# Turning layer inputs and heads in 32x32 blocks on the vector engine, in a two-layer hybrid decoder trunk

## The chip, the cores and the metric

One core of one Trainium2 chip. The metric is the time of one execution on the device, in microseconds (us); of several runs the median counts. Times of single instructions come from one profiled execution. Engines by their names in the profile: PE is the matmul engine, PEld its weight loads, DVE the vector engine, ACT the scalar engine, POOL GpSimd, SP the engine whose queue issues all DMAs here.

## What is computed

A trunk of two layers over x of 2048 rows and 1024 columns, float32. Each layer, cut to what matters:

```
proj = x @ w_in                                   # 1024 -> 3608 columns
dn_q, dn_k, dn_v, dn_z, dn_b, dn_a, g_q, g_k, g_v, g_z, g_r = split(proj)
q, k, v = silu(causal_conv4(dn_q, dn_k, dn_v)); q, k = l2norm(q) / sqrt(128), l2norm(k)
o_dn  = gated_delta_rule(q, k, v, g(dn_a), sigmoid(dn_b))      # 4 heads of 128
o_dn  = rms_norm(o_dn, per head) * dn_norm_g * silu(dn_z)
log_f = log_sigmoid(g_r @ gla_gate_w2 + gla_gate_b) / 16
o_gla = gated_linear_attention(g_q / 8, g_k, g_v, log_f)       # 4 heads, keys 64, values 128
o_gla = rms_norm(o_gla, per head) * gla_norm_g * silu(g_z)
y = concat(o_dn, o_gla) @ w_out                   # 1024 -> 1024
x = layer_norm(alpha * x + y) * ln_g + ln_b       # alpha = 4 ** 0.25
```

Both recurrences carry a state from row to row; the delta rule is computed in chunks of 128 rows with the inverse of a triangular matrix per chunk and head.

## The kernel before

**Tiling.** Each layer is worked off in two halves of 1024 rows (L1341), each half in two blocks of 512 rows (`b`), each block in four chunks of 128 rows (`c`). So there are four halves in all, and eight chunks in each. Every operand of a projection is kept as two float32r parts, `hi` (the rounded value) and `lo` (the rest), and a projection is three products: hi x hi, hi x lo, lo x hi. `proj_group` (L715) makes 24 matmuls of 128x512 for a group of 128 output columns and a block; a half has 24 such groups (four each of delta-rule queries, keys and values, eight of gates, four of the other queries and keys) for each of two blocks. `out_half` (L1287) makes 24 for one chunk and one half of the 1024 output columns.

**The order of the work.** The kernel is first recorded. `Recorder.order` (L238) then simulates the five engines with costs from `_cost` (L477), hands each engine the ready operation with the lowest key (its place in the program, less a lift that a `+n` in `PLAN` gives to a stage), and emits one fixed order for each engine. `HOP` (L465) is the time that the planner counts from the end of an operation on one engine to its use on another. Operations recorded with `either` (copies, scalings, and `subtract` and `product`) go to the engine that would end them sooner. `SLOTS` (L552) gives the number of buffers by tag; a buffer is used again when its last reader is done. In `PLAN` (L558), q, a and b are stages of the linear attention, d, k, i, m, v, y and r those of the delta rule (decay, keys, inverse, its completion, values, queries, recurrence), w the second pair's values, g gates; the digits are the head or pair, and the block. `m4` has 5 buffers of 128x1024 words, `wh` and `wl` 3 each, `xt` 4 (each `hi` or `lo` of a block's inputs, and of half the output weights).

**The inputs.** `load_row` (L726) brings 128 rows as they are, rows on partitions. `prep_xt` (L731) turns them: 8 transposes per chunk on PE against the identity matrix `ident`, into two PSUM banks of tag `tr`; ACT rounds each bank to `hi`, DVE subtracts to `lo`. Partition p of column block k is then contraction row 128k + p, and the weights are loaded likewise (`load_w`, L694; `load_wo`, L1260).

**The heads.** `dn_rec` (L1223, the delta rule) and `gla_long` (L957) leave a head of a block as rows on partitions, scaled by its norm. `finish_head` (L1033) turns it with 4 transposes on PE into a PSUM bank of tag `ch`, and scales it by the gain (per partition by then) into `oT`. `gate` (L1041) projects the head's gate, takes its SiLU, multiplies `oT` by it and sends the product to the DRAM buffer `og`. `split_o` (L1272) brings a chunk of all eight heads back with columns on partitions and splits it to `hi` and `lo` for `out_half`; for chunks 0 to 2 it does so in three pieces, the last of which is head 3 alone, and the matmuls take the heads in the order 4, 5, 6, 7, 0, 1, 2, 3 (L1285). The last three gates are worked off behind the plan (L1430 to L1436), for block 0 and then for block 1.

**The inverse.** `dn_invert` (L1108) builds the 32x32 diagonal blocks of the inverses of all eight chunks of a head on DVE, in `Tb`, with group, chunk and block on partitions. They pass through the DRAM buffer `ud` (L1141 to L1144) to get the layout in which `dn_merge` (L1150) completes the inverse on PE (tag `mg`).

**The recurrence** of a head walks its chunks one by one: two matmuls with the state `Sd`, one with `rr`, two with `vn`, and between them steps on DVE and ACT. Projections of other stages fill PE in between, as the order has it.

Of the kernel before, what the change touches and what calls it, by code (L numbers as in the profile page):

```python
# [464 lines left out]
HOP = {"tensor": 55.0, "vector": 35.0, "scalar": 35.0, "gpsimd": 110.0, "sync": 60.0}  # L465
# [11 lines left out]
def _cost(o, outs, ins):  # L477
# [4 lines left out]
    if o.eng == "tensor":  # L482
# [5 lines left out]
        if lhs.dt == F32R:  # L488
            o.takes = max(w / 2.4 + 14.0, 110.0)
            if o.mode != "r":  # L490
                o.takes = 430.0
        elif o.name == "transpose":
            o.takes = 110.0
        else:
            o.recs = 2
            o.takes = {"32x32": 26.0, "64x32": max(18.0, 0.42 * w), "128x32": max(18.0, 0.42 * w), "64x64": 62.0, "128x64": 113.0,
                       "64x128": 127.0}.get(o.mode, 2 * max(111.5, w * 0.85))
# [37 lines left out]
    else:  # L535
# [17 lines left out]
         "s1": 16, "Sc": 3, "nd": 2, "ud": 2, "og0": 2, "og1": 2, "decd": 2, "bst": 4, "gr": 2, "U32": 1, "T32": 1, "Nd": 2}  # L553
BANKS = {"pj": 2, "tr": 3, "ch": 2, "mg": 1}
LEVELS_MASK = (16, 8, 4, 2, 1)
WHOLE, PARTS = ((0, 8),), ((4, 8), (0, 3), (3, 4))
# [6 lines left out]
def hymba_trunk(ctx: ExitStack, tc, x, w_in, conv_w, dn_a_log, dn_dt_bias, gla_gate_w2, gla_gate_b,  # L563
# [469 lines left out]
    def finish_head(o, gain):  # L1033
        pt = PS([P, NC, P], "ch")
        for c in range(NC):
            nc.tensor.transpose(pt[:, c, :], o[:, c, :], ident)
        oT = T([P, BLK], "m2")
        scaled(oT, pt.rearrange("p c t -> p (c t)"), gain)
        return oT

    def gate(w, xtb, oT, dst):  # L1041
        acc = proj_group(w, xtb)
        y = row2()
        nc.scalar.activation(y, acc, AF.Silu)
        product(oT, oT, y)
        nc.sync.dma_start(dst, oT)
# [61 lines left out]
    def dn_invert(st):  # L1108
# [114 lines left out]
    def dn_rec(h, b, st):  # L1223
# [33 lines left out]
        return finish_head(o, gd)  # L1257


    def load_wo(l, n):  # L1260
        hi = T([P, KT, BLK], "xt", F32R)
        lo = T([P, KT, BLK], "xt", F32R)
        for k in range(0, KT, 2):
            ks = slice(k, k + 2)
            raw = T([P, 2, BLK], "m4")
            nc.sync.dma_start(raw, w_out[l][k * P:(k + 2) * P, n * BLK:(n + 1) * BLK]
                              .rearrange("(k p) c -> p k c", p=P))
# [17 lines left out]
    HEADS = (4, 5, 6, 7, 0, 1, 2, 3)  # L1285

    def out_half(o2, wo, n, y, st):  # L1287
        (oh, ol), (wh, wl) = o2, wo
        acc = PS([P, BLK], "pj")
        for k in HEADS:  # L1290
            nc.tensor.matmul(acc, oh[:, k, :], wh[:, k, :], start=(k == HEADS[0]), stop=False)
            nc.tensor.matmul(acc, oh[:, k, :], wl[:, k, :], start=False, stop=False)
        for k in HEADS:
            nc.tensor.matmul(acc, ol[:, k, :], wh[:, k, :], start=False, stop=(k == HEADS[-1]))
# [16 lines left out]
    def out_proj(l, so, do, src, dst, og, wo, o2):  # L1311
# [7 lines left out]
        for c, n in ((0, 0), (1, 0), (2, 0), (0, 1), (1, 1), (3, 0), (2, 1), (3, 1), (4, 0), (4, 1), (5, 0), (5, 1),  # L1319
                     (6, 0), (7, 0), (6, 1), (7, 1)):  # L1320
            if n == 0:
# [3 lines left out]
                if c not in o2:  # L1325
                    o2[c] = split_o(c, og, WHOLE)
# [7 lines left out]
    for l in range(depth):  # L1334
# [6 lines left out]
        for hf in range(n_half):  # L1341
# [8 lines left out]
            og = [DR([8, P, BLK], f"og{b}") for b in range(NB)]  # L1350
# [4 lines left out]
            if l == 0 and hf == 0:  # L1355
                with lifted(600):
                    early = {0: load_row(src, 0)}
            wv0 = load_v(l, 0, True)
            for b in range(NB):
                with lifted(150):  # L1360
                    xt.append(prep_xt(lambda c: early.pop(b * NC + c, None) or load_row(src, so + b * BLK + c * P)))
# [23 lines left out]
            oT = {}  # L1385

            def g2(p, b):
                os_ = gla_long(gl[p, b], v[p, b], Sg[p])
                for h in range(2):
                    oT[4 + 2 * p + h, b] = finish_head(os_[h], gg)  # L1390

            def gates(e):
                w = load_group(l, (GZ0 + P * (e - 4)) if e > 3 else Z0 + P * e)
                for b in range(NB):
                    gate(w, xt[b], oT[e, b], og[b][e])
# [14 lines left out]
            def rec_block(h, b):  # L1410
                oT[h, b] = dn_rec(h, b, dn[h])
# [18 lines left out]
            z = [(e, load_group(l, Z0 + P * e)) for e in (1, 2, 3)]  # L1430
            for e, w in z:
                gate(w, xt[0], oT[e, 0], og[0][e])
            wo = [load_wo(l, 0)]
            o2 = {0: split_o(0, og, PARTS)}
            for e, w in z:
                gate(w, xt[1], oT[e, 1], og[1][e])  # L1436
            for c in (1, 2):
                o2[c] = split_o(c, og, WHOLE if c > 2 else PARTS)
            wo.append(load_wo(l, 1))
            out_proj(l, so, do, src, dst, og, wo, o2)  # L1440
# [27 lines left out]
```

## Time and profile before

| | |
|---|---|
| runs shown (3) | 2171.54, 2171.9, 2174.57 us; median 2171.9 |
| profiled execution | 2170.34 us |
| its span, first to last instruction | 2168.6 us |
| granted clock of PE | 0.998 |
| busy: PE, PEld, DVE, ACT, POOL | 98%, 82%, 65%, 53%, 23% of the span |
| moved by DMA | 215.40 MB, 279267 packets |

How to read it: a group row gives line, engine, operation, the tiles written and read by the program's names (`m` stands for the buffers of both `m2` and `m4`, `s` for small ones), the shape and the count; behind the bar, the time in which the group was busy, the mean duration of one instruction in ns, and the idle time of its engine just before them with what ended it. Every instruction is emitted at L433, so tiles, not lines, tell the groups apart. A transpose on PE reads as a matmul that has `ident` as an operand. A float32 matmul that is not a transpose counts twice, for it is made of two records. A timeline row gives the start and the duration in us; merged instructions have a count. Matmuls overlap, so the spacing of their starts and not the duration tells what each takes from PE.

### The profile page before, as it was taken

How to read it: one execution, taken by the hardware profiler on the slowest of the kernel's cores; microseconds unless marked ns; L12 is line 12 of the kernel's file. 1: busy time of each engine (PE TensorE's matmuls, PEld its weight loads, DVE VectorE, ACT ScalarE, POOL GpSimd, SP SyncE). 2: the span in 40 equal slices, each digit the busy share in tenths (PEclk: the TensorE clock that was granted, in tenths of full speed). 3: DMA queues.
4: the chain of work that ended last, by engine and by line, in shares of the span. 5: the costliest groups of instructions: out<-in, count | busy, mean ns of one | idle time of the engine just before them, and what ended most of it. 6: DMA issues, size and time to landing. Idle time of an engine off the chain costs nothing.

```text
span 2168.6 us, 45520 instructions
## 1 busy us (share of the span) xinstructions
PE 2122.9 (98%) x17426; PEld 1779.1 (82%) x17426; DVE 1408.5 (65%) x3311; ACT 1157.3 (53%) x3253; POOL 495.2 (23%) x877
## 2 busy tenths in 40 slices
PE   8999999999999999999999999999999999999998
PEld 7887878788998788878888878887889887888787
DVE  4567777656456777755645677776564567777556
ACT  4676756441457675643145767565315576656520
POOL 3342112111134211211113421111111341212110
PEclk9999999999999999999999999999999999999999
DMA  4222332373221332236322143324732213332461
GB/s 140 70 61 81 105 86 67 102 220 122 89 69 51 96 110 71 72 109 215 123 87 60 50 115 96 81 57 119 223 112 81 67 48 108 96 80 57 126 190 58
DMA packets 279267, 215.40 MB, mean 99 GB/s; under 512 B 69828, under 2 KB 225800, under 8 KB 279048
## 3 DMA queue, kind: packets, MB, share of 16 engines
q1 hardware_dynamic: 279048, 212.48, 33.3%
q8 instruction: 137, 2.24, 0.4%
q14 instruction: 82, 0.67, 0.1%
HBM read 166.23 MB, written 46.20 MB: 98 GB/s over the span
## 4 chain that ended last, share of the span: by engine, by line
PE 85%; DMA 5%; DVE 5%; ACT 2%; issue 1%; POOL 1%; DVEq 0%; SPq 0%; POOLq 0%
PE pj L433 65%; PE ch L433 9%; PE tr L433 8%; DMA ud<-Tb 4%; PE mg L433 2%; DMA U<-ud 1%; ACT m L433 1%; DVE m L433 1%; DVE kq L433 1%; DVE wl L433 1%; DVE tmp L433 1%; DVE R L433 0%; POOL s L433 0%; DVE s L433 0%; DVE Tb L433 0%
## 5 line engine op out<-in xcount | busy, mean ns | idle before, releaser
L433 PE MATMUL pj<-xt,wh 128*128 128x512 f32 x4096 | 1090.5, 402 | 2.1 <-ACT wh L433 2.1
L433 PEld LDWEIGHTS pj<-xt,wh 128*128 128x128 f32 x4096 | 742.9, 189 | 141.3 <-ACT wh L433 3.0
L433 PE MATMUL pj<-xt,wl 128*128 128x512 f32 x2048 | 568.4, 401 | 0.0
L433 PEld LDWEIGHTS pj<-xt,wl 128*128 128x128 f32 x2048 | 374.4, 189 | 69.0 <-issue 0.2
L433 PE MATMUL pj<-wh,xt 128*128 128x256 f32 (+1 forms) x1024 | 196.6, 290 | 1.5 <-ACT wh L433 1.5
L433 POOL TENSOR_TENSOR s<-s,mhalf 128x4 f32<-128x4 f32 (+2 forms) x80 | 103.3, 1292 | 334.3 <-DVE s L433 333.5
L433 PEld LDWEIGHTS pj<-wh,xt 128*128 128x128 f32 x1024 | 162.2, 190 | 2.4 <-ACT wh L433 1.9
L433 ACT CAST wh<-wr 128x1024 fp32r<-128x1024 f32 (+2 forms) x116 | 118.0, 1024 | 86.0 <-PE pj L433 62.6
L433 DVE SCALAR_TENSOR_TENSOR kq<-raw,cw,kq 128x512 f32<-128x512 f32 x192 | 146.5, 765 | 3.7
L433 DVE TENSOR_TENSOR wl<-wr,wh 128x512 fp32r<-128x512 f32 (+2 forms) x170 | 119.4, 733 | 21.3 <-ACT wh L433 11.8
L433 PE MATMUL pj<-wl,xt 128*128 128x280 f32 (+1 forms) x512 | 131.3, 289 | 0.9 <-DVE wl L433 0.5
L433 DVE TENSOR_TENSOR m<-m,m 128x256 f32<-128x256 f32 (+1 forms) x244 | 114.4, 490 | 19.8 <-ACT m L433 5.5
L433 DVE SCALAR_TENSOR_TENSOR m<-m,pj 128x512 f32<-128x512 f32 x64 | 43.9, 685 | 121.9 <-PE pj L433 121.9
L433 ACT CAST wh<-m 128x1024 fp32r<-128x1024 f32 (+3 forms) x56 | 37.3, 679 | 159.3 <-PE pj L433 148.8
L433 POOL MEMSET m<- 128x512 f32 (+1 forms) x160 | 79.0, 508 | 90.1 <-PE tr L433 56.7
L433 POOL TENSOR_TENSOR wl<-wr,wh 128x512 fp32r<-128x512 f32 (+2 forms) x42 | 61.2, 1466 | 167.7 <-ACT wh L433 126.7
L433 PEld LDWEIGHTS pj<-wl,xt 128*128 128x128 f32 x512 | 97.6, 191 | 1.6 <-DVE wl L433 0.8
L433 POOL COPY halo<-raw 128x3 f32<-128x3 f32 x96 | 20.4, 213 | 341.7 <-ACT raw L433 299.0
L433 PEld LDWEIGHTS ch<-Sd,kq 128*128 128x128 f32 x512 | 78.4, 190 | 23.6 <-DVE Sd L433 13.4
L433 ACT COPY m<-m 64x256 f32<-64x256 f32 (+1 forms) x198 | 78.0, 411 | 23.1 <-PE tr L433 11.3
L433 PE MATMUL ch<-Sd,kq 128*128 128x128 f32 x512 | 87.1, 278 | 3.2 <-DVE Sd L433 2.7
L433 DVE SCALAR_TENSOR_TENSOR Sd<-Sd,eg,ch 128x128 f32<-128x128 f32 x128 | 44.2, 345 | 69.2 <-PE ch L433 68.0
(193 smaller groups left out, 3407.9 us busy)
## 6 DMA issues: line engine op xcount, KB each, us to landing
wr<-in_w_in_dram SPq DMA_DIRECT2D x104, 512.0 KB
m<-decd SPq DMA_DIRECT2D x64, 256.0 KB
og<-m SPq DMA_DIRECT2D x64, 256.0 KB
m<-in_w_out_dram SPq DMA_DIRECT2D x32, 512.0 KB
m<-og SPq DMA_DIRECT2D x20, 512.0 KB
m<-in_x_dram SPq DMA_DIRECT2D x16, 512.0 KB
m<-gr SPq DMA_DIRECT2D x32, 256.0 KB
decd<-m SPq DMA_DIRECT2D x32, 256.0 KB
```

Source lines behind the costliest of these rows:

```text
L433: getattr(getattr(self.nc, o.eng), o.name)(*[real(a) for a in o.args], **{k: real(a) for k, a in o.kw.items()})
```

## The change

Inputs, heads and weights meet in another order of the 1024 contraction rows: partition p of column block k now holds row 8p + k (`rows_of`). The inputs come in four DMAs for each chunk, one for each 256 columns, onto 32 partitions each: partition 32a + t holds, for each of the four groups of 32 rows, columns 256a to 256a + 255 of row t of the group. One `transpose` instruction on DVE turns all 32x32 blocks of a chunk (`turned`); it reads every eighth word and writes in sequence. ACT's rounding and the subtraction read its output, and the subtraction may now be on DVE or POOL. PE's transposes of the inputs are gone.

Heads go to DRAM as they are (`finish_head` is one DMA), into `og`, by pairs; gates, with the gain multiplied in, go to a DRAM buffer of their own, `zg`. `split_o` loads a chunk's heads in the form of the inputs, turns them likewise on DVE, loads the chunk's gates, multiplies, and splits. Heads and gates no longer wait for each other before DRAM, the pieces of `split_o` are gone, and the matmuls take the column blocks in order. PE's transposes of the heads are gone.

`ud` gets an order in which the write is contiguous in each partition. The planner counts 300 ns instead of 55 for a hop to PE, and 42 ns for a matmul of 64 by 32; `PLAN` has another order and other lifts.

```diff
-HOP = {"tensor": 55.0, "vector": 35.0, "scalar": 35.0, "gpsimd": 110.0, "sync": 60.0}
+HOP = {"tensor": 300.0, "vector": 35.0, "scalar": 35.0, "gpsimd": 110.0, "sync": 60.0}
...
-            o.takes = {"32x32": 26.0, "64x32": max(18.0, 0.42 * w), "128x32": max(18.0, 0.42 * w), "64x64": 62.0, "128x64": 113.0,
+            o.takes = {"32x32": 26.0, "64x32": 42.0, "128x32": max(18.0, 0.42 * w), "64x64": 62.0, "128x64": 113.0,
...
-PLAN = ("q0 w d1 a00 b00 a01 d0+400 b01 q1+50 a10 b10 k0 v0 g4+50 a11 i0 g5 b11 m0+50 y0 r00 k1 d2 y1 d3 "
-        "i1 g7 r01+50 g6 k2 m1 v1 r10 r11+600 v2 i2 k3 y2 m2 r20 r21 v3 y3 i3+50 m3+200 r30 r31+250 g0+100")
+LAST = 1, 2, 3
+PLAN = ("q0+50 w a00 d0+200 b00+50 d1 a01 q1 a10 b01 d2 k0 v0 b10+100 g4 a11 i0 b11+700 y0+100 g5 m0 k1+500 d3+200 r00 k2 "
+        "y1 r01 v1 i1 m1+50 k3 g6 r10 y2 i2 m2+400 v2+450 r11+1050 r20+50 r21 v3+100 g7+400 i3+150 g0 m3+650 y3+50 r30+300 r31+250")
...
+    def rows_of(src):
+        return src.rearrange("(p k) c -> p k c", p=P)
+
+    def turned(raw):
+
+
+        out = T([P, NC, KT, 32], "m4")
+        nc.vector.transpose(out, raw.rearrange("p b (i k) -> p b k i", k=KT))
+        return out.pattern(0, [(32, KT), (32 * KT, NC), (1, 32)])
...
-                nc.sync.dma_start(raw[:, :, at:at + w],
-                                  src[k0 * P:(k0 + n_k) * P, c0:c0 + w].rearrange("(k p) c -> p k c", p=P))
+                nc.sync.dma_start(raw[:, :, at:at + w], rows_of(src)[:, k0:k0 + n_k, c0:c0 + w])
...
-    def load_row(src, t):
-        row = T([P, D], "m4")
-        nc.sync.dma_start(row, src[t:t + P, :])
-        return row
+    def load_rows(src, t):
+        raw = T([P, NC, 2 * P], "m4")
+        for a in range(4):
+            nc.sync.dma_start(raw[32 * a:32 * a + 32], src[t:t + P, 256 * a:256 * a + 256].rearrange("(b t) e -> t b e", b=4))
+        return raw
...
         for c in range(NC):
-            row = rows(c)
-            pts = []
-            for kk in range(0, KT, 4):
-                pt = PS([P, 4, P], "tr")
-                for j in range(4):
-                    nc.tensor.transpose(pt[:, j, :], row[:, (kk + j) * P:(kk + j + 1) * P], ident)
-                pts.append(pt)
-            for kk, pt in zip(range(0, KT, 4), pts):
-                h = hi[:, kk:kk + 4, c * P:(c + 1) * P]
-                nc.scalar.copy(h, pt)
-                nc.vector.tensor_tensor(out=lo[:, kk:kk + 4, c * P:(c + 1) * P], in0=pt,
-                                        in1=h.bitcast(F32), op=ALU.subtract)
+            xt = turned(rows(c))
+            parts = lambda t: t[:, :, c * P:(c + 1) * P].rearrange("p k (b t) -> p k b t", b=4)
+            nc.scalar.copy(parts(hi), xt)
+            subtract(parts(lo), xt, parts(hi).bitcast(F32))
...
-    def finish_head(o, gain):
-        pt = PS([P, NC, P], "ch")
-        for c in range(NC):
-            nc.tensor.transpose(pt[:, c, :], o[:, c, :], ident)
-        oT = T([P, BLK], "m2")
-        scaled(oT, pt.rearrange("p c t -> p (c t)"), gain)
-        return oT
-
-    def gate(w, xtb, oT, dst):
+    def finish_head(o, dst):
+        nc.sync.dma_start(dst.rearrange("(c t) e -> t c e", c=NC), o)
+
+    def gate(w, xtb, gain, dst):
         acc = proj_group(w, xtb)
         y = row2()
         nc.scalar.activation(y, acc, AF.Silu)
-        product(oT, oT, y)
-        nc.sync.dma_start(dst, oT)
+        scaled(y, y, gain)
+        nc.sync.dma_start(dst, y)
...
-        ud = DR([NCH, 4, 8, 4, 32], "ud")
-        nc.sync.dma_start(ud.rearrange("c r s g i -> g (c r) s i"), Tb)
+        ud = DR([4, NCH, 4, 8, 32], "ud")
+        nc.sync.dma_start(ud.rearrange("g c r s i -> (g c r) (s i)"), Tb.rearrange("p s i -> p (s i)"))
         U32 = T([P, NCH, 32], "U32")
-        nc.sync.dma_start(U32, ud.rearrange("c r s g i -> (r s g) c i"))
+        nc.sync.dma_start(U32, ud.rearrange("g c r s i -> (r s) g c i"))
...
-    def split_o(c, og, parts):
+    def split_o(c, og, zg):
 
         b, cs = c // NC, slice((c % NC) * P, (c % NC + 1) * P)
-        gl = T([P, KT, P], "m4")
+        raw = T([P, NC, 2 * P], "m4")
+        for a in (2, 3, 0, 1):
+            nc.sync.dma_start(raw[32 * a:32 * a + 32], og[b][a, cs, :].rearrange("(b t) e -> t b e", b=4))
+        z = T([P, KT, P], "m4")
+        nc.sync.dma_start(z, zg[b].rearrange("h c t -> (h c) t").rearrange("(p k) t -> p k t", k=KT)[:, :, cs])
+        ot = turned(raw)
+        z4 = z.rearrange("p k (b t) -> p k b t", b=4)
+        product(z4, ot, z4)
         oh = T([P, KT, P], "wh", F32R)
         ol = T([P, KT, P], "wl", F32R)
-        for e0, e1 in parts:
-            es = slice(e0, e1)
-            nc.sync.dma_start(gl[:, es, :], og[b][es, :, cs].rearrange("h p t -> p h t"))
-            nc.scalar.copy(oh[:, es, :], gl[:, es, :])
-            subtract(ol[:, es, :], gl[:, es, :], oh[:, es, :].bitcast(F32))
+        nc.scalar.copy(oh, z)
+        subtract(ol, z, oh.bitcast(F32))
         return oh, ol
```

The rest follows from these: `load_wo` uses `rows_of`, `out_half` takes k from 0 to 7, `dn_rec`, `g2`, `gates` and the calls behind the plan pass `og` and `zg` where they passed `oT`, and `SLOTS` has two DRAM buffers for each of `zg0` and `zg1`.

More of the change, by code (lines that the diff above doesn't have):

```diff
@@ L552 @@
 SLOTS = {"xt": 4, "wh": 3, "wl": 3, "wr": 2, "m4": 5, "m2": 20, "kq": 9, "raw": 2, "sq": 2, "rr": 2, "qs": 2, "vn": 2,
-         "s1": 16, "Sc": 3, "nd": 2, "ud": 2, "og0": 2, "og1": 2, "decd": 2, "bst": 4, "gr": 2, "U32": 1, "T32": 1, "Nd": 2}
+         "s1": 16, "Sc": 3, "nd": 2, "ud": 2, "og0": 2, "og1": 2, "zg0": 2, "zg1": 2, "decd": 2, "bst": 4, "gr": 2, "U32": 1, "T32": 1, "Nd": 2}
 BANKS = {"pj": 2, "tr": 3, "ch": 2, "mg": 1}
 LEVELS_MASK = (16, 8, 4, 2, 1)
-WHOLE, PARTS = ((0, 8),), ((4, 8), (0, 3), (3, 4))
-PLAN = ("q0 w d1 a00 b00 a01 d0+400 b01 q1+50 a10 b10 k0 v0 g4+50 a11 i0 g5 b11 m0+50 y0 r00 k1 d2 y1 d3 "
-        "i1 g7 r01+50 g6 k2 m1 v1 r10 r11+600 v2 i2 k3 y2 m2 r20 r21 v3 y3 i3+50 m3+200 r30 r31+250 g0+100")
+LAST = 1, 2, 3
+PLAN = ("q0+50 w a00 d0+200 b00+50 d1 a01 q1 a10 b01 d2 k0 v0 b10+100 g4 a11 i0 b11+700 y0+100 g5 m0 k1+500 d3+200 r00 k2 "
+        "y1 r01 v1 i1 m1+50 k3 g6 r10 y2 i2 m2+400 v2+450 r11+1050 r20+50 r21 v3+100 g7+400 i3+150 g0 m3+650 y3+50 r30+300 r31+250")
 @with_exitstack
@@ L1221, in dn_queries, with dn_rec @@
         k["qT"], k["sq"] = qT, sq_
-    def dn_rec(h, b, st):
+    def dn_rec(h, b, st, dst):
         k, S = st["b"][b], Sd[h]
@@ L1256, in dn_rec @@
             scaled(o[:, c, :], o[:, c, :], ssq[:, c:c + 1])
-        return finish_head(o, gd)
+        finish_head(o, dst)
     def load_wo(l, n):
@@ L1265, in load_wo @@
             raw = T([P, 2, BLK], "m4")
-            nc.sync.dma_start(raw, w_out[l][k * P:(k + 2) * P, n * BLK:(n + 1) * BLK]
-                              .rearrange("(k p) c -> p k c", p=P))
+            nc.sync.dma_start(raw, rows_of(w_out[l])[:, k:k + 2, n * BLK:(n + 1) * BLK])
             nc.scalar.copy(hi[:, ks, :], raw)
@@ L1289, in out_half @@
         acc = PS([P, BLK], "pj")
-        for k in HEADS:
-            nc.tensor.matmul(acc, oh[:, k, :], wh[:, k, :], start=(k == HEADS[0]), stop=False)
+        for k in range(KT):
+            nc.tensor.matmul(acc, oh[:, k, :], wh[:, k, :], start=(k == 0), stop=False)
             nc.tensor.matmul(acc, oh[:, k, :], wl[:, k, :], start=False, stop=False)
-        for k in HEADS:
-            nc.tensor.matmul(acc, ol[:, k, :], wh[:, k, :], start=False, stop=(k == HEADS[-1]))
+        for k in range(KT):
+            nc.tensor.matmul(acc, ol[:, k, :], wh[:, k, :], start=False, stop=(k == KT - 1))
         nc.vector.scalar_tensor_tensor(out=y, in0=y, scalar=alpha, in1=acc, op0=ALU.mult, op1=ALU.add)
@@ L1309, in norm_rows, with out_proj @@
             nc.sync.dma_start(dst[:, cs], y)
-    def out_proj(l, so, do, src, dst, og, wo, o2):
+    def out_proj(l, so, do, src, dst, og, zg, wo, o2):
         lng, lnb = [], []
@@ L1325, in out_proj @@
                 if c not in o2:
-                    o2[c] = split_o(c, og, WHOLE)
+                    o2[c] = split_o(c, og, zg)
                 sts[c] = T([P, 2, 6], "bst")
@@ L1349, in hymba_trunk @@
                 nc.gpsimd.memset(sm[:, :, 33:34], 1.0)
-            og = [DR([8, P, BLK], f"og{b}") for b in range(NB)]
+            og = [DR([4, BLK, 2 * P], f"og{b}") for b in range(NB)]
+            zg = [DR([8, P, BLK], f"zg{b}") for b in range(NB)]
             decd = DR([4 * NB, P, BLK], "decd")
@@ L1356, in hymba_trunk @@
                 with lifted(600):
-                    early = {0: load_row(src, 0)}
+                    early = {0: load_rows(src, 0)}
             wv0 = load_v(l, 0, True)
@@ L1360, in hymba_trunk @@
                 with lifted(150):
-                    xt.append(prep_xt(lambda c: early.pop(b * NC + c, None) or load_row(src, so + b * BLK + c * P)))
+                    xt.append(prep_xt(lambda c: early.pop(b * NC + c, None) or load_rows(src, so + b * BLK + c * P)))
                 if b == 0 and hf == 0:
@@ L1383, in g1 @@
                 gla_short(gl[p, b])
-            oT = {}
             def g2(p, b):
@@ L1389, in g2 @@
                 for h in range(2):
-                    oT[4 + 2 * p + h, b] = finish_head(os_[h], gg)
+                    finish_head(os_[h], og[b][2 + p, :, h * P:(h + 1) * P])
             def gates(e):
@@ L1394, in gates @@
                 for b in range(NB):
-                    gate(w, xt[b], oT[e, b], og[b][e])
+                    gate(w, xt[b], gg if e > 3 else gd, zg[b][e])
             dn = {}
@@ L1410, in rec_block @@
             def rec_block(h, b):
-                oT[h, b] = dn_rec(h, b, dn[h])
+                dn_rec(h, b, dn[h], og[b][h // 2, :, h % 2 * P:(h % 2 + 1) * P])
             def values(h):
@@ L1429, in hymba_trunk @@
                     stage[name[0]](*(int(n) for n in name[1:]))
-            z = [(e, load_group(l, Z0 + P * e)) for e in (1, 2, 3)]
+            z = [(e, load_group(l, Z0 + P * e)) for e in LAST]
             for e, w in z:
-                gate(w, xt[0], oT[e, 0], og[0][e])
+                gate(w, xt[0], gd, zg[0][e])
             wo = [load_wo(l, 0)]
-            o2 = {0: split_o(0, og, PARTS)}
+            o2 = {0: split_o(0, og, zg)}
             for e, w in z:
-                gate(w, xt[1], oT[e, 1], og[1][e])
+                gate(w, xt[1], gd, zg[1][e])
             for c in (1, 2):
-                o2[c] = split_o(c, og, WHOLE if c > 2 else PARTS)
+                o2[c] = split_o(c, og, zg)
             wo.append(load_wo(l, 1))
-            out_proj(l, so, do, src, dst, og, wo, o2)
+            out_proj(l, so, do, src, dst, og, zg, wo, o2)
         cur = nxt
```

1 line of the change is left out of this document (removed).

## The prediction

> **What bounds the kernel now.** I read the page first, for which engine is full.
>
> ```profile
> span 2168.6 us, 45520 instructions
> ...
> PE 2122.9 (98%) x17426; PEld 1779.1 (82%) x17426; DVE 1408.5 (65%) x3311; ACT 1157.3 (53%) x3253; POOL 495.2 (23%) x877
> ...
> q1 hardware_dynamic: 279048, 212.48, 33.3%
> ```
>
> TensorE is busy for 2122.9 of 2168.6 us: 45.7 us idle in all. No other engine is above 65%, and the DMA engines stand at a third. A busy PE need not be a full one, so next I looked in the timeline of PE at what one instruction adds to the next one's start.
>
> ```profile
> 528.85 0.48 PE L433 MATMUL pj<-xt,wh 128*128 128x512 f32 x1
> 529.16 0.27 PE L433 MATMUL tr<-ident,m 128*128 128x128 f32 x1
> 529.19 0.48 PE L433 MATMUL pj<-xt,wh 128*128 128x512 f32 x1
> 529.50 0.27 PE L433 MATMUL tr<-ident,m 128*128 128x128 f32 x1
> ...
> 114.40 2.66 PE L433 MATMUL pj<-xt,wh 128*128 128x512 f32 x11
> 116.90 0.60 PE L433 MATMUL tr<-ident,m 128*128 128x128 f32 x4
> 117.25 0.95 PE L433 MATMUL pj<-xt,wh 128*128 128x512 f32 x3
> 118.13 0.30 PE L433 MATMUL tr<-m,m 64*32 64x64 f32 x2
> ```
>
> The chain of waits shows the pace of projections alone:
>
> ```profile
> 2072.05 88.90 PE pj L433 x392
> ```
>
> 88.90/392 is 0.227 us for a projection matmul. One of these and one transpose take 0.34 us (529.16 to 529.50), so a transpose takes 0.113 us of PE's time. In a group of four between projections it is (118.13 - 114.40 - 14 x 0.227)/4 = 0.14 us. PE goes from one to the next without a gap: it is the bound, and work taken off it shortens the kernel as long as the others keep up.
>
> **What the change removes.** The groups of instructions carry the two kinds of transposes, and what feeds on them:
>
> ```profile
> L433 PE MATMUL tr<-ident,m 128*128 128x128 f32 x448 | 71.3, 280 | 5.9 <-POOL lm L433 4.5 <-DMA m<-in_x_dram 1.1 <-DVE xt L433 0.4
> L433 PE MATMUL ch<-ident,m 128*128 128x128 f32 x256 | 50.5, 279 | 7.2 <-DVE m L433 7.2
> L433 DVE TENSOR_TENSOR xt<-tr,xt 128x512 fp32r<-128x512 f32 x64 | 41.6, 686 | 15.9 <-ACT xt L433 15.5
> L433 DVE STREAM_TRANSPOSE T<-Nd 128x256 f32<-128x256 f32 x16 | 7.1, 444 | 3.1 <-ACT Nd L433 2.8
> L433 DVE TENSOR_TENSOR xt<-m,xt 128x1024 fp32r<-128x1024 f32 x32 | 39.0, 1218 | 1.1 <-ACT xt L433 1.0
> L433 POOL TENSOR_TENSOR m<-m,m 128x512 f32<-128x512 f32 x28 | 42.3, 1511 | 188.1 <-ACT m L433 188.1
> L433 ACT ACTIVATE m<-ch,gd 128x512 f32<-128x512 f32 x32 | 21.9, 686 | 12.9 <-PE ch L433 12.9
> ```
>
> Layer inputs: 8 transposes per 128 rows, 8 such chunks per half sequence, 4 halves (two per layer, two layers): 256 of the 448 in the first row. At 0.113 us that is 28.9 us. Heads: all 256 of the second row. At 0.113 us they are 28.9 us, and the row also shows 7.2 us in which PE stood before them waiting for the scaled head; together 36.1, which agrees with 256 x 0.14 = 35.8. I take 28.9 + 35.8 = 64.7 us off PE, all on the path.
>
> The mean duration, 279 ns, is not the price, because these instructions overlap. The Trainium skill (TensorE: Matmul & The Clock Gate, Part 4: PE-mode transpose) gives about 275 ns for a transpose within a kernel. The duration here agrees with it, the spacing does not, and by it the sum would be 141 us instead of 64.7, and the time 2030.
>
> **The inversion's round trip through DRAM.** `ud` is laid out so that each partition writes one run of 1 KB instead of eight of 128 bytes; its reading back stays in 128-byte runs. In the chain of waits of one inversion, and in PE's own waits:
>
> ```profile
> 206.89 4.79 DMA ud<-Tb
> 211.70 2.32 DMA U<-ud
> ```
>
> ```profile
> PE mg L433 <- DVE T L433: 12.4, 8, 2.8
> ...
> PE pj L433 <- ACT wh L433: 3.6, 5, 1.5
> ```
>
> The write takes 4.79 us, the read 2.32. With fewer pieces I put the write at the read's 2.32. The 12.4 us are PE's waits for the block that this pair brings, 8 of them, the longest 2.8 us; 2.5 us earlier removes nearly all. Bounds 0 (another step is late next) and 12.4; I take 8. What is late next is Tb itself, which the vector engine builds row by row.
>
> **What it adds on the vector engine.** 32 transposes of 128x1024 for the inputs and 32 for the heads. The trace has only 128x256, contiguous, at 444 ns. With 1218 - 686 = 532 ns for 512 more elements of a subtraction (1.04 ns each), 128x1024 is 444 + 768 x 1.04 = 1.24 us, 79 us in all. But the new form reads every eighth word, 32 bytes apart, and no row shows that. Lower bound 1.24 us; upper bound twice that, 2.48, if every element needs two reads. I take 1.24, since the transpose here already runs at the pace of a two-input subtraction. The other edits nearly cancel: 64 subtractions at 0.69 (41.6 us) become 32 at 1.22 (39.0); ACT's casts of the inputs have the same number of elements; the gain multiplies the gate (64 of about 0.69 us) where it multiplied the head (64 of 0.69); the product of gate and head has as many elements as before, partly on POOL (28 at 1.5 us). Engine totals: DVE about 1490 of 2105 us, 71%. The cover is that PE has other work; the question is the out projection, where half of these transposes and the next half's inputs meet.
>
> ```profile
> core 0: us, PE busy (x) PEld busy (x) DVE busy (x) ACT busy (x) POOL busy (x), PEclk, DMA share, GB/s
> ...
> 405.00:461.00 56.00, 53.23 (x382) 42.44 (x381) 28.24 (x70) 30.31 (x94) 11.84 (x8) 1.00 0.58 179
> ...
> 455.00:575.00 120.00, 120.00 (x628) 102.84 (x628) 71.25 (x119) 28.64 (x54) 18.05 (x18) 1.00 0.45 145
> ```
>
> In 455 to 575 DVE has 71.2 us. Take away 16 subtractions (11.0), add 16 transposes (19.8), 8 subtractions and 8 products at 1.22 (19.5): 99.5 us if POOL takes none, against 120 less the 4 us of PE's own transposes. It fits, with POOL 85% idle to take part. At 2.48 us each it would be 119 of 116: full.
>
> **DMAs.** Added pieces: heads out 64 x 512 = 32,768 of 512 bytes; heads in 32 x 512 = 16,384 of 1 KB; inputs 4 KB rows in four (+12,288); `ud` -14,336; the gates' way out and in replaces the old one's piece for piece. Sum +47,000. The page's 33.3% of 16 x 2168.6 us over 279,048 pieces is 41 ns each, so +1.9 ms over 16 engines, 120 us or 6 points of share: 39%. In 405 to 575, now 45 to 58%, perhaps 65%. SP's queue gets 264 more issues (64 heads out, 96 for inputs, 104 for heads and gates in). An issue is
>
> ```profile
> 458.80 0.38 SPq L433 DMA_DIRECT2D m<-in_w_out_dram  x1
> ```
>
> 0.38 us, so 100 us in 2100; what queues behind them on SP are the weight loads, which are issued well ahead (PE's wait for `wh`, 3.6 us in all, above). Dealing the contraction rows out anew costs the weights nothing that I can see: as many pieces of the same length.
>
> The path from the last head of block 0 to the first out matmul loses 4 transposes (0.5) and a scaling (0.69) and gains a transpose (1.24) and a product (1.22): +1.3 us per half, 5 us in all, if the gates' matmuls in between do not cover it (they do now). I count 5 in full, as the price of new waits. At the start the same: PE's 4.5 us before its first transpose (the wait for POOL's `lm`) goes, and the load in four pieces plus 1.24 us on DVE takes its place; zero, with 3 us either way.
>
> **Sum.** The profiled execution took 2170.3 us, its span 2168.6; the median of the runs shown is 2171.9, 1.6 above. 2170.3 - 64.7 - 8 + 5 = 2102.6, in median terms 2104.
>
> **The rivals.** *The order hides more.* The planner now counts 300 ns where it counted 55 between another engine's result and PE, so it puts more projections between dependent matmuls. What there is to win:
>
> ```profile
> PEld ch L433 <- DVE Sd L433: 13.4, 45, 1.0
> PEld ch L433 <- ACT vn L433: 12.2, 57, 0.3
> ...
> PEld ch L433 <- DVE rr L433: 7.8, 41, 0.3
> ```
>
> These waits of the weight loads sum to 33 us, and part of them reaches PE; half of that gone makes 2104 - 17 = 2087. Against: the same projections are now wanted for hiding in fewer places only if they do not run out.
>
> *They run out: slower.* The projections that fill PE between the steps of the delta rule are a fixed stock, and the plan, its lifts and the 300 ns spend it earlier. A step of the recurrence today:
>
> ```profile
> 451.79 0.71 PE L433 MATMUL ch<-Sd,kq 128*128 128x128 f32 x4 [0.49 <-DVE Sd L433]
> 452.25 0.71 PE L433 MATMUL pj<-xt,wh 128*128 128x512 f32 x2
> 452.80 0.41 PE L433 MATMUL ch<-rr,m 128*128 128x128 f32 x2
> ...
> 453.75 0.69 PE L433 MATMUL ch<-vn,m 128*128 128x128 f32 x4
> ...
> 454.98 0.61 PE L433 MATMUL ch<-Sd,kq 128*128 128x128 f32 x4
> ```
>
> From 451.79 to 454.98, 3.19 us, of which about 1.1 (0.46 + 0.22 + 0.44) is its own; 2.1 us are filled by projections, or else idle. If the last head's 8 steps per half are left bare, that costs 4 x 8 x 2.1 = 67 us, all the gain. The point from which it decides is those 8 steps; at 10 the time is 2104 + 84 = 2188. For it: PE already idles 2.8 of 56 us in 405 to 461. Against: gates no longer wait for their heads, which loosens the fill.
>
> *The vector engine becomes the bound in the out projection.* With transposes at 2.48 us, DVE's order is 20 us behind per out projection, and the next half's inputs come late by some 7 us at each of four seams, with as much as 3 more at the start: 2104 + 31 = 2135. The Trainium skill (SBUF — State Buffer, Door 1: The DMA port swizzle) says that SBUF works in 16-byte lines and that an access that crosses to a new line each time pays a penalty, at no stated price. By that rule this rival holds, since 32 bytes lie between reads; no run here shows it.
>
> *No gain.* The freed PE slots reappear as waits for DMAs in 405 to 575, where the share grows most: 16 us at each of four seams, 2170. That needs landings several times the 2.3 to 4.8 us above.
>
> **How the numbers follow.** Forecast 0.58, range 2092 to 2115 by the bounds (0 to 12.4 for `ud`, 0 to 5 for new waits, 3 for the start). More hidden: 0.12. DVE bound: 0.20. Fill runs out: 0.07. No gain: 0.03. The range, 2084 to 2140, takes in the first three. A measurement tells about 0.2% (4 us) from no change. Faster 0.90, same 0.03, slower 0.07.
>
> **What would show it.** Right: no `ident` matmuls on `ch`, 192 on `tr`, PE busy near 2060 and still near 98%, 64 stream transposes of 128x1024 at about 1.24 us, `ud<-Tb` near 2.3 us, no `mg` wait for T. Wrong: transposes of 2 us or more with PE waiting for `xt` or `wh` after the out projections; PE idle in the last stretch of the recurrences on `Sd`, `vn` and `rr`; or PE waits put down to loads of `og` or `zg`.

## The result, and the profile after

The median of 4 runs is 2137.2 us (2135.0 to 2139.6), before it was 2172.2: ratio 0.984, 95% interval [0.982, 0.985], 35 us faster. The profiled execution took 2139.6 us. In the same views as before, first the page:

```profile
span 2137.5 us, 44695 instructions
...
PE 2071.0 (97%) x16914; PEld 1748.3 (82%) x16914; DVE 1544.3 (72%) x3275; ACT 1160.3 (54%) x3249; POOL 483.1 (23%) x837
...
q1 hardware_dynamic: 330568, 246.05, 41.0%
```

TensorE gave up 512 transposes and 51.9 us of busy time. The span fell by only 31.1: idle time of PE went from 45.7 to 66.5 us. The groups that answer to those of before:

```profile
L433 DVE STREAM_TRANSPOSE m<-m 128x1024 f32<-128x1024 f32 x64 | 137.1, 2145 | 34.5 <-DMA m<-og 23.8 <-DMA m<-in_x_dram 10.1 <-DMA m<-xs 0.6
...
L433 PE MATMUL tr<-ident,m 128*128 128x128 f32 x192 | 31.2, 275 | 0.0
```

The new transpose takes 2.145 us, not 1.24. PE's own waits, in total (us), number and longest:

```profile
PE pj L433 <- ACT sm L433: 15.7, 7, 8.8
PE pj L433 <- DVE m L433: 13.5, 13, 2.5
PE pj L433 <- ACT wh L433: 11.2, 5, 9.1
```

The row for the inversion's T is gone. At the top stand matmuls that write `pj`. Of the wait for `wh`, 9.1 us are the one before the very first projection; the other four, some 0.5 us each, stand at the end of the start and of the seams. (A seam is the stretch from one half's out projection into the next half.) The other two rows are waits for a PSUM bank: `pj` has two, `sm<-pj` is a copy on ACT that empties one, and in the out projection `m<-m,pj` on DVE does, which adds the matmuls' result to the input. The timelines of DVE and PE show the second kind, a bank that is emptied late because a transpose stands before it in DVE's order:

```profile
523.87 2.06 DVE L433 STREAM_TRANSPOSE m<-m 128x1024 f32<-128x1024 f32 x1
525.85 0.64 DVE L433 SCALAR_TENSOR_TENSOR m<-m,pj 128x512 f32<-128x512 f32 x1
...
526.64 3.68 PE L433 MATMUL pj<-xt,wh 128*128 128x512 f32 x15 [2.03 <-DVE m L433]
```

Before others of these waits it is steps of the layer norm or a subtraction that stand there. How the stretches look (columns as in the prediction's table of stretches):

```profile
0.00:30.00 30.00, 10.02 (x49) 8.98 (x49) 18.59 (x23) 8.33 (x10) 18.64 (x69) 0.94 0.82 194
...
30.00:40.00 10.00, 8.11 (x46) 8.11 (x47) 9.59 (x9) 3.92 (x8) 1.79 (x1) 0.66 0.25 68
...
455.00:575.00 120.00, 115.39 (x569) 98.11 (x568) 107.07 (x123) 26.01 (x35) 19.43 (x17) 0.99 0.60 170
...
480.00:540.00 60.00, 57.97 (x254) 47.13 (x253) 58.67 (x73) 8.05 (x8) 11.33 (x10) 1.00 0.49 149
```

In the first 30 us PE works for 10. In 455 to 575, where DVE had 71 us, it has 107, and in the middle 60 us it is full at 58.67. The chain of waits from 480 to 580 us shows the vector engine as what ends last, until PE takes over:

```profile
by line: PE pj L433 33.9%; DVE m L433 33.5%; issue 12.2%; DMA m<-og 7.0%; DVE wl L433 5.3%; DVE xt L433 3.7%; DVE bst L433 3.6%; DMA m<-in_x_dram 3.6%; DVE bmv L433 1.1%; ACT wh L433 1.1%; DVE s L433 0.8%; DVEq L433 0.3%; ACT sm L433 0.2%; 
```

### The profile page after: what moved, and what is told of

Read it like the earlier page. It is cut to its first block, busy times and chain, and to the rows that moved or that the text cites. A ratio compares the mean times of both kernels' runs of the same rounds, so it can differ in the third digit from the quotient of the medians.

```text
span 2137.5 us, 44695 instructions
## 1 busy us (share of the span) xinstructions
PE 2071.0 (97%) x16914; PEld 1748.3 (82%) x16914; DVE 1544.3 (72%) x3275; ACT 1160.3 (54%) x3249; POOL 483.1 (23%) x837
## 4 chain that ended last, share of the span: by engine, by line
PE 70%; DVE 12%; DMA 9%; ACT 4%; issue 3%; SPq 1%; POOL 1%; DVEq 0%; ACTq 0%; POOLq 0%
PE pj L433 54%; PE ch L433 9%; DVE m L433 7%; PE tr L433 6%; DMA m<-og 4%; DMA m<-zg 2%; PE mg L433 2%; ACT m L433 2%; DVE wl L433 1%; DMA m<-in_x_dram 1%; SPq L433 1%; DVE bst L433 1%; DVE kq L433 1%; DMA m<-xs 1%; POOL m L433 1%
## 5 line engine op out<-in xcount | busy, mean ns | idle before, releaser
L433 PE MATMUL pj<-xt,wh 128*128 128x512 f32 x4096 | 1062.0, 400 | 15.9 <-DVE m L433 12.3
L433 PE MATMUL pj<-xt,wl 128*128 128x512 f32 x2048 | 552.0, 400 | 5.1 <-DVE wl L433 3.6
L433 DVE STREAM_TRANSPOSE m<-m 128x1024 f32<-128x1024 f32 x64 | 137.1, 2145 | 34.5 <-DMA m<-og 23.8
L433 ACT CAST wh<-wr 128x1024 fp32r<-128x1024 f32 (+2 forms) x116 | 118.0, 1024 | 59.6 <-PE pj L433 44.4
L433 DVE TENSOR_TENSOR m<-m,m 128x256 f32<-128x256 f32 (+1 forms) x237 | 128.9, 564 | 25.7 <-ACT m L433 9.4
L433 ACT CAST wh<-m 128x1024 fp32r<-128x1024 f32 x32 | 33.7, 1052 | 206.0 <-DVE m L433 130.3
L433 DVE TENSOR_TENSOR wl<-wr,wh 128x512 fp32r<-128x512 f32 (+3 forms) x166 | 117.9, 742 | 7.6 <-ACT wh L433 5.3
L433 ACT CAST xt<-m 128x1024 fp32r<-128x1024 f32 x64 | 66.5, 1047 | 83.3 <-PE pj L433 35.9
L433 ACT COPY m<-m 64x256 f32<-64x256 f32 (+1 forms) x232 | 90.3, 410 | 12.7 <-PE tr L433 4.8
L433 POOL TENSOR_TENSOR wl<-wr,wh 128x512 fp32r<-128x512 f32 (+1 forms) x46 | 66.2, 1443 | 115.5 <-ACT wh L433 57.1
L433 PEld LDWEIGHTS ch<-Sd,kq 128*128 128x128 f32 x512 | 77.1, 190 | 12.6 <-DVE Sd L433 2.2
L433 ACT ACTIVATE m<-m,s 128x128 f32<-128x128 f32 x199 | 65.6, 391 | 38.4 <-DVE s L433 24.7
```

Source lines behind the costliest of these rows:

```text
L433: getattr(getattr(self.nc, o.eng), o.name)(*[real(a) for a in o.args], **{k: real(a) for k, a in o.kw.items()})
```

## The experiments

The theory after the first look: taking transposes off PE gained little, because DVE at 2.145 us each becomes the bound at the seams and the inputs come late at the start; the 35 us come largely from two edits that move no transpose, `ud` and the planner's 300 ns. The rival: the move gained its 64.7 us, and something else in the change lost 30. Each ratio is to runs of the kernel before on the same chip.

**What the step costs the vector engine.** The kernel after, with unused work added at its start: transposes of 128x1024 at steps of 1, 2, 4, 8, 16 and 32 words, products at 1, 2, 4 and 8, and two small transposes.

```
+    for s in (1, 2, 4, 8, 16, 32):
+        nc.vector.transpose(mo.rearrange("p (g k i) -> p g k i", i=32, k=s), mi.rearrange("p (g i k) -> p g k i", i=32, k=s))
+    for s in (1, 2, 4, 8):
+        nc.vector.tensor_tensor(out=..., in0=mi.rearrange("p (g i k) -> p g k i", i=32, k=s), ...)
```

> The changed kernel with a row of extra vector-engine instructions ahead of everything: transposes of a 128x1024 constant tile that read every 1st, 2nd, 4th, 8th, 16th and 32nd word, products of two such tiles at steps 1, 2, 4 and 8, and transposes of 128x256 at steps 1 and 8. Only their durations count; the start is some 20 us later. Theory that the step of the read sets the price: 128x1024 takes about 1.24 us at step 1 and near 2.0 to 2.15 at step 8, and at 128x256 0.44 against about 0.7. Rival, that the length or DMA traffic at the same time makes the 2.14 us seen in the changed kernel: all steps alike.

The timeline of DVE, start and duration, shows the six (with two of the kernel's own among the later rows), then the products in their order:

```profile
1.93 1.25 DVE L433 STREAM_TRANSPOSE m<-m 128x1024 f32<-128x1024 f32 x1
3.21 1.25 DVE L433 STREAM_TRANSPOSE m<-m 128x1024 f32<-128x1024 f32 x1
4.49 1.99 DVE L433 STREAM_TRANSPOSE m<-m 128x1024 f32<-128x1024 f32 x1
6.39 1.97 DVE L433 STREAM_TRANSPOSE m<-m 128x1024 f32<-128x1024 f32 x1
...
20.00 1.28 DVE L433 TENSOR_TENSOR m<-m,m 128x1024 f32<-128x1024 f32 x1
25.38 1.18 DVE L433 TENSOR_TENSOR m<-m,m 128x1024 f32<-128x1024 f32 x1
29.65 1.96 DVE L433 TENSOR_TENSOR m<-m,m 128x1024 f32<-128x1024 f32 x1
32.66 2.05 DVE L433 TENSOR_TENSOR m<-m,m 128x1024 f32<-128x1024 f32 x1
```

Two transposes take 1.25 us, the rest 1.96 to 2.02, and the products have the same edge: free at 4 and 8 bytes, 0.7 to 0.8 us dearer at 16 bytes, and hardly more beyond (products to 32 bytes, transposes to 128). The transposes of 128x256 take 0.45 us in sequence and 0.66 at a step of 32 bytes. It is the step, not the transpose. That fits the rule of the Trainium skill's SBUF — State Buffer (Door 1: The DMA port swizzle), four fp32 words being one line; the page has no price, these rows have it. In the kernel, beside other work, it is 2.145.

**The same, read in order.** Contraction rows are dealt out in blocks of 32, so that every transpose reads its words in sequence; loads of weights and gates then come in four pieces of 32 partitions.

```
-        return src.rearrange("(p k) c -> p k c", p=P)
+        return src.rearrange("(a k i) c -> a i k c", a=4, k=KT)[a]
...
-        nc.vector.transpose(out, raw.rearrange("p b (i k) -> p b k i", k=KT))
+        nc.vector.transpose(out, raw.rearrange("p b (k i) -> p b k i", k=KT))
...
+                for a in range(4):
+                    nc.sync.dma_start(raw[32 * a:32 * a + 32, :, at:at + w], rows_of(src, a)[:, k0:k0 + n_k, c0:c0 + w])
```

> Contraction rows dealt so that the transpose reads words in sequence: partition 32a + i of column block k holds row 256a + 32k + i. The weights' and gates' loads then need four DMAs of 32 partitions each where one did; pieces and bytes are the same. Theory that the step of the read makes the vector engine the bound in the out projections: transposes 1.24 us instead of 2.14, DVE busy less by 58 us, PE idle per half down by 3 to 4 us in the two middle halves and by some 5 in the first 58 us, time 2115 to 2125 (changed kernel 2137). Rival, the price comes from length or traffic: transposes stay near 2.1 us and the time is 2137 or more, by the added DMA issues on SP. Second rival, vector engine is not what PE waits for: transposes are short, time within 4 us of 2137.

2144.8 us, 0.9875 [0.986, 0.989]: slower than the change by some 8 us. The group row of its transposes and the largest wait of PE:

```profile
L433 DVE STREAM_TRANSPOSE m<-m 128x1024 f32<-128x1024 f32 x64 | 78.9, 1238 | 70.1 <-DMA m<-og 44.2 <-DMA m<-in_x_dram 19.3 <-DMA m<-xs 4.2
```

```profile
PE pj L433 <- ACT xt L433: 17.0, 1, 17.0
```

The duration is the 1.24 of the prediction, 58 us are off DVE, and the time is no better. DVE now waits for loads. SP issues 40 pieces of weights where 6 loads stood ahead of the second inputs, and the first half reaches a fixed place (its first transpose of `sm` on PE) at 71.5 us for 58.5. From one such place to the next it is then 2.9 us longer than the change, 4.1 shorter and 7.0 shorter, and after the last one 6.7 longer. (The profiled execution, 2150.8 us, is the slowest of its five.) The transposes are short, as the theory had it, but its time of 2115 to 2125 is missed. The length of the transposes is not all of it, and with a start that got worse this run cannot show what it is worth.

**A planner that knows the price.** The change, with 2145 ns in the planner for this transpose.

```
+        if o.name == "transpose" and n == 1024:
+            o.takes = 2145.0
```

> The changed kernel, with only the planner's cost of a 128x1024 transpose set from 1.23 to 2.145 us, so that the order is made with what the chip takes. Theory that the order is wrong because the planner counts too little: POOL takes more of the subtractions and products, PE idle per half falls by 3 to 4 us, time about 2125. Theory that the vector engine lacks the time, whatever the order: within 6 us of 2137, either way.

2130.0 us, 0.981 [0.979, 0.982]: 7 us better than the change. The planner hands 12 subtractions of the inputs to POOL, where it handed it 2. That lies between the two expectations: PE's idle time falls by 3.4 us in all, not in each half, and its busy time by 3.7.

**The start alone.** The first half's inputs go back to PE, all other transposes stay on DVE.

```
+            on_pe = l == 0 and hf == 0
...
+                        nc.tensor.transpose(pt[:, j, :], row.pattern(kk + j, [(KT, P)]), ident)
```

> The changed kernel, but the inputs of the very first half are turned on PE as before (64 transposes, one load per chunk; their stationary operand is read at every eighth word, so that the contraction rows stay as the change deals them). Theory that half of what is missing lies in the first 58 us, where no other work covers loads, transposes and rounding in turn: PE idle in the first 60 us falls from 23.7 to about 9, PE does 7 us more, time 2137 - 15 + 7 = 2129. Rival, that the start waits for DMAs in any case: idle stays near 20, time 2137 to 2144.

2126.0 us, 0.979 [0.978, 0.980]: 10.6 us better than the change by the ratios. The start in stretches:

```profile
0.00:30.00 30.00, 23.11 (x145) 21.17 (x146) 15.50 (x32) 14.27 (x28) 17.10 (x69) 1.00 0.71 217
```

PE works 23.1 of the first 30 us instead of 10.0, at full clock, and its idle time in the first 60 us falls from 23.7 to 7.4 (9 expected). At the start PE has nothing else to do, so its transposes were free there.

**The edits that move no transpose, each alone on the kernel before.**

```
-HOP = {"tensor": 55.0, "vector": 35.0, "scalar": 35.0, "gpsimd": 110.0, "sync": 60.0}
+HOP = {"tensor": 300.0, "vector": 35.0, "scalar": 35.0, "gpsimd": 110.0, "sync": 60.0}
```

> The kernel before with one edit: the planner counts 300 ns for a hop to PE where it counted 55. Theory that the longer hop hides PE's small waits in the recurrence: PE's waits on Sd, vn, rr and T fall, time 2172 - 10 to 20. Rival, that the hop matters only with the rest of the change, or not at all: within 4 us of 2172. If the fill of projections runs out: slower than 2176.

2159.7 us, 0.993 [0.991, 0.996]: 14.8 us from the planner's 300 ns alone, as expected in size. Of the waits that the expectation names, those of PE for T fall from 12.4 to 6.0 us and for `Sd` from 2.7 to nothing, while those for `vn` and `rr` rise to 4.3 and 1.1; the 7.2 us for the heads (`ch` on `m`) go as well. And `ud` alone, its three lines as in the change's diff:

> The kernel before with the new layout of ud alone: the write takes 1.7 to 2.3 us instead of 4.8. Theory of the prediction: PE's 12.4 us of waits for T go, time 2172 - 8 = 2164. Rival, that another step is late next or that the read gets slower by what the write gains (in the changed kernel the read's landing is 4.2 us): within 4 us of 2172.

2157.7 us, 0.992 [0.990, 0.994]: 16.8 us. DMAs of `ud`, KB and us to landing:

```profile
ud<-Tb SPq DMA_DIRECT2D x16, 128.0 KB, 1.7
U<-ud SPq DMA_DIRECT2D x16, 128.0 KB, 2.7
```

The write lands in 1.7 us (median; 3.5 in the run with both edits); on the chain of the kernel before, writes of `ud` took from 4.69 to 7.81. PE's 12.4 us of waits for T fall to 0.9. The time is better than either expectation. Both together:

> The kernel before with both edits that move no transpose: the new layout of ud and 300 ns between engines in the planner. Alone they gave 16.8 and 14.8 us. If they add up: 2172 - 31.6 = 2140.6, and the move of the transposes as a whole is worth only the 3 us that are left of the change's 35. If both take away the same waits of the inversion and the recurrence: 2150 to 2156, and the move is worth 13 to 19 us. If my sum on record were right in its term of 64.7 us, this kernel could not be under 2160.

2142.5 us, 0.985 [0.983, 0.987]: the two add up (-31.6 expected, -32.8 by the ratio). Its page, still with all 512 transposes on PE:

```profile
span 2139.3 us, 45535 instructions
...
PE 2116.1 (99%) x17426; PEld 1793.5 (84%) x17426; DVE 1416.4 (66%) x3309; ACT 1147.0 (54%) x3244; POOL 501.0 (23%) x888
```

This kernel is within the interval of the change itself, 0.982 to 0.985. Moving the transposes and the new list of steps are together worth 2 us or nothing. The rival could only stand if the new list lost what the move gained.

**The order taken out of the change.** The change with the old HOP, the old price of `64x32` and the old list of steps.

> The changed kernel with the planner's old numbers: hop to PE 55 ns, the old price of a 64x32 matmul and the old PLAN. What is left is the change of data flow alone. Theory that the gain comes from PE's missing transposes: most of the 35 us is there, time 2137 to 2150. Rival, that the new order makes the gain and the transposes give nothing: time 2165 to 2175.

2153.8 us, 0.990 [0.988, 0.993], between the two expectations: 14 us of the change's 35 go with the order, as in the kernel before. Against `ud` alone (2157.7), measured beside it, this kernel differs by the move of the transposes alone, in the old list: 4 us, and the intervals overlap. So it is not the new list that hides a gain of 60 us, and the rival falls. The new list alone on the kernel before was not run.

**Heads and inputs apart.** The change with all layer inputs on PE (the edit of the start, for all halves); the heads stay on DVE.

> The changed kernel with the inputs of all four halves turned on PE; only the heads are turned on the vector engine. Against the run that puts the first half's inputs back, PE does 192 transposes more, 22 us, and the vector engine 48 transposes of 2.15 us less. Theory that the vector engine is the bound in the out projections: PE idle in the two middle halves falls from about 10 to about 5 us each, time 2126 + 22 - 15 = 2133. Rival, that PE does not wait for the vector engine there: 2126 + 22 = 2148.

2122.7 us, 0.976 [0.975, 0.978], better than either expectation. So, by the ratios: from both edits alone to this kernel, heads on DVE, -19 us (the new list of steps included); from this kernel to the change, inputs on DVE, +16 us, of which 10.6 are the first half's (the run with the start alone) and 6 those of the other three halves, where the two intervals still overlap a little. Its page:

```profile
span 2118.9 us, 45117 instructions
...
PE 2087.3 (99%) x17170; PEld 1771.4 (84%) x17170; DVE 1479.1 (70%) x3276; ACT 1165.4 (55%) x3284; POOL 467.7 (22%) x833
```

256 transposes less than the kernel with both edits and 28.8 us less PE: 0.113 us each, the prediction's price. When the other 256 come off too, in the change, PE's busy time falls by only 16.3 us, at a clock of 0.993 for 0.999, and its idle time rises by 35 (31.6 to 66.5). PE's waits for `m` on DVE are 2.8 us here, 13.5 in the change, and 13.0 with only the first half's inputs on PE: it is the move of the later inputs that makes DVE empty the banks late.

**Better versions.** The last kernel with the planner's 2145 ns:

> The kernel after with its layer inputs turned on TensorE (2122.7 before this edit) and the planner's cost of a block transpose of 128x1024 set to the measured 2.145 us. If the wrong cost in the planner is what makes its order poor, it gains here too, though only the 32 transposes of the heads are left: half of the 7 us that it gave with all 64, 2119. If it was the inputs' transposes that the wrong cost misplaced, nothing changes: 2122 to 2124.

2118.5 us, 0.974 [0.972, 0.975], the fastest of all; against the 0.976 without the price the intervals overlap a little, so 4 us are likely and not sure. Then the heads read in order, out weights and gates loaded in four pieces:

```
+            for a in range(4):
+                nc.sync.dma_start(raw[32 * a:32 * a + 32],
+                                  w_out[l].rearrange("(a k i) c -> a i k c", a=4, k=KT)[a, :, k:k + 2, n * BLK:(n + 1) * BLK])
```

> As the last one, but the heads alone are dealt out so that their transpose reads its words in order (1.24 us each, and the planner is told so), at the price of loads of the out weights and of the gates in four pieces. If the length of the transposes in the out projection is what still costs: 32 x 0.9 = 29 us less on the vector engine, 3 to 8 us less in time, 2113 to 2118. If the vector engine no longer decides there once the inputs are off it: no gain, 2121 to 2125, and more if the four loads in place of one come late.

2143.6 us, 0.985 [0.984, 0.987]: 25 us slower than the one before. (The load of the gates is split in the same way, and the planner counts 1240 ns.) The transposes take 1243 ns, but DVE's product of head and gate waits 24.0 us for loads of `zg` (5.4 before), and its transposes of the heads wait 32.2 us for `og` (24.5). Then without the four pieces: the gates stored in the dealt order, the out weights in two loads of 128 partitions.

```
+            for j in range(2):
+                nc.sync.dma_start(raw[:, j, :], w_out[l].rearrange("(a k i) c -> k a i c", a=4, k=KT)[k + j, :, :, n * BLK:(n + 1) * BLK])
...
+                    gate(w, xt[b], gg if e > 3 else gd, zg[b][e // 2, :, 4 * (e % 2):4 * (e % 2) + 4, :].rearrange("i k t -> k i t"))
```

> The heads again dealt out so that their transpose reads in order, the layer inputs on TensorE, but without loads in four pieces of 32 partitions: the gates are stored in the dealt order, so that their load is one again, and the out weights come in two loads of all 128 partitions where the last run had four of 32. If the four pieces were what cost the last run its 25 us: all of that comes back, and the faster transposes (1.24 us for 2.145) now show, 2110 to 2118. If the new dealing itself or the planner's changed order costs: 2135 to 2145 again.

2277.7 us, 1.048 [1.047, 1.050]: both expectations missed. The chain of waits at its first out projection:

```profile
439.76 11.89 DMA m<-in_w_out_dram
451.71 8.05 DMA zg<-m
460.45 8.24 DMA zg<-m
468.75 7.75 DMA zg<-m
485.84 15.49 DMA m<-in_w_out_dram
```

256 KB take 8 to 15 us here, where the fastest kernel's 512 KB loads of the out weights land in 5.7 and its 256 KB stores of gates in 4.2 (medians; the one such store on its chain took 6.2). The pieces are of 2 KB in both. What differs is the order of the pattern on the DRAM side: its slowest dimension has 4 entries here, 128 there. The Trainium skill (DMA: Bandwidth & Descriptors, Rules for kernel authors) says that this dimension sets how many of the 16 DMA engines a transfer uses, so 4 here; the durations fit it, which engines moved the bytes no view here shows. Queueing behind one another is in these times too: in the same run writes of `ud`, whose layout is the change's, took 9.6 to 10.0 us on the chain. So the test of the four pieces was spoilt by a worse load, and whether pieces or their order cost the 25 us stays open.

## Why the prediction came out near, and where it was wrong

The time lies in the range, 3 us from its end, and near the rival in which the vector engine becomes the bound (2135). The forecast itself, 2104 and at most 2115, missed: 35 us came where 68 were expected. And the sum is not what happened:

| term | predicted, us | measured by runs, us |
|---|---|---|
| heads to DVE | -35.8 and +5 of waits | -19 (new list of steps included) |
| inputs to DVE | -28.9, start 0 +/- 3 | +16, of it 10.6 at the start |
| `ud` | -8 (0 to -12.4) | -16.8 |
| 300 ns in the planner | 0 (rival: -17) | -14.8 |
| sum | -67.7 | -35 |

**The price of a transpose on PE** (0.113 us) held: 28.8 us of PE for 256.

**"64.7 us off PE, all on the path" is the step that failed**: the two moves together gave 3 us, by the table. It failed in three ways. First, the term of 1.24 us: 2.145, because the step of 32 bytes was costed by a row of sequential reads. The bound of 2.48 and the rule on 16-byte lines were in the text; the value between them was chosen by the wrong row. What these 0.9 us each cost in time no run separates: all three runs with 1.24 us came out slower, with loads that came late. Second, at the start there is no other work for PE to cover the move, and "zero, 3 us either way" was far off: the first half's inputs, forecast to give 7.2 us (64 transposes), cost 10.6. There the chain of waits up to 60 us holds loads of `x` for 29.4% and SP's issues for 11.7%. PE's wait of 8.8 us there is for a bank that ACT empties late: ACT waited 5.3 us for the small load of `nega` and 1.8 for a later chunk's transpose, and the copy stood behind them in its order. (Why the loads are issued so late, by SP's four pieces or by the five `m4` buffers, of which each chunk now takes two, was not tested, nor was another order on ACT.) Third, part of the 35.8 for heads, the 7.2 us in which PE stood before them, was not the transposes' to give: with `ud` and the 300 ns alone that row shows 1.4, all transposes still in place.

**Where the 57.6 us of the transposes went.** The kernel with both small edits and the change differ by the move alone (and the list of steps). The table of stretches, cut at PE's first transpose of `sm` in each half, first for that kernel, then for the change:

```profile
0.00:48.44 48.44, 41.20 (x272) 38.29 (x273) 19.02 (x42) 19.04 (x43) 16.52 (x68) 1.00 0.46 139
...
578.37:1109.58 531.21, 528.83 (x4359) 447.47 (x4358) 350.46 (x819) 289.17 (x820) 123.74 (x214) 1.00 0.34 101
```

```profile
0.00:58.46 58.46, 34.80 (x209) 32.63 (x210) 33.32 (x42) 17.94 (x34) 21.04 (x70) 0.91 0.48 115
...
582.49:1110.80 528.31, 517.08 (x4231) 435.63 (x4230) 388.25 (x816) 290.66 (x816) 121.12 (x201) 1.00 0.42 118
```

At the start PE's idle time goes from 7.2 to 23.7 us. From cut to cut it goes from 2.6, 2.4 and 2.2 to 8.0, 11.2 and 11.7, and after the last cut from 8.9 to 11.9: 26.8 us more over four seams. The prediction's rival had 7 at each of four seams, 28, and 3 at the start: the seams were priced well and the start was not. For DVE from 455 to 575 us the forecast had 99.5 us and the rival 119; it was 107, and full in the middle 60.

Part of the rest is the clock. Its mean is 0.993 in the change and 0.999 in the other, but where PE stands still a low clock costs nothing. Weighted by PE's busy time, in stretches of 2 us, the change loses 8.9 us and the other nothing, an estimate. In sum -57.6 + 16.4 + 26.8 + 8.9 = -5.5, and the two spans differ by 1.8: 3.7 us stay open. Less clock is granted where PE has stood still: 0.66 from 30 to 40 us, into which the gap reaches that this row of PE's timeline ends.

```profile
31.89 0.60 PE L433 MATMUL pj<-wh,xt 128*128 128x280 f32 x1 [8.76 <-ACT sm L433]
```

PE had stopped at 23.1 us. Cut finer, the clock is 1.00 up to 26.4 us and 0.50 from 26.6 to 36.5. The Trainium skill (TensorE: Matmul & The Clock Gate, Part 1: The HAM clock gate) has half the clock after an idle window of about 3.4 us; the trace agrees, it fell some 3.4 us after the stop. It was back 4.6 us after PE went on, so this wait cost some 2.3 us more than its own length.

**The terms for `ud` and the order** were too small by half and by all. `ud` was bounded by PE's 12.4 us of waits, and the profiled execution with it alone is 15.5 shorter: idle time fell by 12.6, and PE's busy time by 2.9 besides. The old write also had 4 entries in the slowest dimension of its DRAM pattern, the new one has 128; whether that or the length of the pieces made the write shorter was not separated. The rival "the order hides more" had a chance of 0.12 and a price of 17 us, and 14.8 came from the 300 ns. The waits of weight loads by which it was priced did go: of 33 us, 1.5 are left, for `Sd` (those for `vn` on DVE, which it did not price, rose from 2.9 to 6.0). But in the profiled execution of that run, 10.5 us shorter, PE's idle time fell by 8.1, and what fell among PE's own waits is chiefly T and the heads, so the size came out near partly by luck. The loss that the rival on fill feared did not come: PE waits 0.9 us in all for `rr` in the change, and `Sd` and `vn` are in no row.

**Luck.** That 2137 is near 2135 is in part luck. The small edits gave 23.6 us more than the sum has for them; the start (13.4 us more than the rival had), the clock (8.9) and the 7.2 us before the heads' transposes, which the small edits had taken already, took about as much away.

**What was to show it.** 192 `ident` on `tr` and none on `ch`, PE busy for 2071.0 us (2060 forecast), 41% DMA share (39 forecast), no wait for T: right. Of the sign named for the prediction being wrong, the transposes of 2 us or more are there. The waits that were to come with them, for `xt` or `wh` behind the out projections, are not: `xt` has 0.3 us, and `wh` some 0.5 at each seam, as before. PE waits there for the banks that DVE and ACT empty late, the path that the prediction did not have.

## What to carry to other kernels

Count the bytes between reads before pricing a vector instruction, and price it by a row with that step. Work taken off the bound is worth its slots only where that engine has other work ready: at the start the same move cost time, and at the seams the inputs' part of it gained none. Look, too, at what else the engine that takes the work does for the bound one: here it empties the PSUM banks into which PE writes, in one fixed order. When one change holds several edits, run the small ones alone first: here they were nearly all of the gain, and the large one had a half that paid and a half that undid it.

## What the runs showed of the hardware

A read step of 16 bytes or more costs the vector engine 0.7 to 0.8 us per 128x1024 of fp32, in a transpose and a product alike, and 8 bytes cost nothing. Transposes at steps of 64 and 128 bytes, 1.96 to 2.02 us, are no worse than at 16 (1.99). Loads of 256 KB whose DRAM pattern has 4 entries in its slowest dimension took 12 to 15 us on the chain of waits; loads of 512 KB with 128 entries there have a median of 5.7, with pieces of 2 KB in both. What of this is queueing was not separated. A gap of 1.9 us on PE at a seam was followed by a granted clock of 0.83 over 10 us in one half (560 to 570 us) and of 1.00 in another (1620 to 1630).
